# Expert outputs of the small blocks: sums in SBUF by one-hot products in place of scatter-adds to DRAM

## The chip, the core and the metric

The kernel runs on one core of one Trainium2 chip. The metric is the device time of one execution in microseconds (us). Three runs of the kernel before took 1320.86, 1321.10 and 1316.58 us, median 1320.86. One further execution was profiled: its own time was 1310.08 us and the span of its trace, from the first to the last instruction, 1308.3 us. All rows below come from that execution, and times inside the kernel are counted from the start of the span. Engines are called as in the profile: PE (matrix products, with PEld for the loading of their stationary operand), DVE (vector), ACT (scalar), POOL (GpSimd) and SP, which here only issues transfers. PE's granted clock of 1.0 is 2.4 GHz; the other level is half of it, so 0.74 in a window is a mean of the two.

## What is computed

One encoder layer on 512 tokens of width 1024, all in fp32: a layer norm; a mixer (sparse attention and differential attention); a cross attention into 256 memory tokens; and a mixture of experts, with a layer norm after each. The change touches the last part only:

```
scores = sigmoid(x @ router_w);  top_e = top 8 of scores + bias
gates  = scores[top_e] / sum * 2.5
y[t]   = sum over the 8 experts e of t:  gate * ((silu(x Wg[e]) * (x Wu[e])) @ Wd[e])
y[t]  += shared expert of t
out    = layer_norm(ALPHA * x + y)
```

There are 64 routed experts, each with three weights of 1 MiB (gate and up 1024 x 256, down 256 x 1024). All 64 are read in every run, about 201 MB of the 325 MB that the kernel moves.

## The kernel before

The experts are sorted by how many tokens chose them. Rank r gets a fixed room of CAPS[r] rows: 128 to 160 for the first ranks, then 112, 96 and 80, then 64 rows for 19 experts (ranks 38 to 56) and 48 rows for 7 (ranks 57 to 63). Ranks 4 and 5 have room for 160 rows and are two blocks each, one of 128 and one of 32 rows. So there are 66 blocks. They run in the order of rank, except that the two big experts are put in at the places BIG_AT = (30, 50) of the order of experts: the first among the experts of 80 rows, the second among those of 64. Tokens beyond the rooms would go through a loop at the end (`tc.For_i`, line 1590) whose count is read at run time and is zero here.

A block begins with a gather: POOL issues an indirect transfer that fetches the block's rows from DRAM (`gather`, line 1218), two blocks ahead. Transposes on PE turn them (`expert_x`, or `narrow_x` in blocks of up to 64 rows), then come gate and up products, the gate on ACT (line 1299), the product with the gate weight on DVE (hm, line 1304), a transpose of that (`expert_h`), and the down product. Blocks of more than 64 rows ("wide") split weights and rows into a high and a low fp32r part on ACT and DVE and take three products for each (`mm3`, lines 101 to 103). Blocks of at most 64 rows ("narrow", 26 of them) use plain fp32, with gate and up side by side on the two halves of the output partitions (`narrow_mm`, line 1280), and the two halves of the down product likewise (`narrow_out`, line 1291). ACT copies the down product into y (line 1294), and POOL issues an indirect transfer with addition into the DRAM tensor acc, 4 KB a row (`scatter`, line 1332). Rows of the room that hold no token go to spare rows of acc. Each scatter waits until the one before it has landed. acc already holds ALPHA * x plus the shared expert.

Weights are loaded by SP in the order of the blocks (`fetch`, `top_up`), up to LEAD = 9 loads ahead of the one in use. Weights, y, the norm's parameters and most other large tiles share one pool of 20 slots of 8 KB a partition (`slot`); a load can be issued once the slot that it was given has been left by its former tile. Products go to 8 PSUM banks (`bank`).

The order of the work on each engine is the order in which the generators of the code are stepped: `schedule` steps them by the times that they yield. In the last part only `experts` is left, which hands narrow blocks to `narrow_block` (line 1494): six of eight k steps of the products; the transpose of the former block's hm; the last two k steps; the gate; the former block's down product and scatter (`finish`); this block's hm; the transposes of the next block's rows.

After the blocks the overflow loop is passed, the four 128-row tiles of acc are read back (line 1625), normed (lines 1627 to 1641, tiles 1 and 3 with their statistics on ACT) and stored.

Of the kernel before, what the change touches and what calls it, by code (L numbers as in the profile page):

```python
# [10 lines left out]
F32 = mybir.dt.float32  # L11
F32R = mybir.dt.float32r
# [7 lines left out]
P = 128  # L20
# [19 lines left out]
AHEAD, LEAD = 2, 9  # L40
BIG_AT = (30, 50)
GRP = 4
# [16 lines left out]
def encoder_layer(  # L59
# [1222 lines left out]

    def narrow_out(m, ht, wd, n):

        if m % 2 == 0:
            Y["y"] = slot([P, 2, D], name="y")
        y = Y["y"][:, m % 2, :]
        ps = bank()
        for j in range(2):
            for c in range(2):  # L1290
                nc.tensor.matmul(ps[HALF * c:HALF * c + n, :], lhsT=ht[:, j, 0:n], rhs=wd[:, j, c * 512:(c + 1) * 512],
                                 start=j == 0, stop=j == 1)
        for c in range(2):
            nc.scalar.copy(y[0:n, c * 512:(c + 1) * 512], ps[HALF * c:HALF * c + n, :])
        return y

# [97 lines left out]
    metas = [[(r, r, 0) for r in range(a, b)] for a, b in [(0, 2), (2, FIX)]] + metas  # L1394
    NB = len(blocks)
    W, XG, GS = {}, {}, {}

# [83 lines left out]
    def finish(m, ht, n, wd, si):  # L1481
        if narrow(m):
            y = narrow_out(m, ht, wd, n)
        else:
            for c in range(2):
                y = expert_out(m, ht, wd, c, n)
        scatter(y, si, n)

# [5 lines left out]
    def narrow_block(m, X, xt, gs, si):  # L1494
        r, _, n, _ = blocks[m]
        step = 3 * step_of[r]
        ps = bank()
        w = W[r]
        narrow_mm(xt, w, n, ps, range(KH))
        yield 0.45 * KH, 0.0  # L1500
        ht = expert_h(*BEFORE[0][0:2])
        narrow_mm(xt, w, n, ps, range(KH, KD))
        yield 0.9, 0.0
        top_up(step + 2)
        sg = expert_gate(ps, n)
        finish(m - 1, ht, *BEFORE[0][1:])
        yield 1.8, 0.0
        BEFORE[0] = expert_mid(sg, ps[HALF:HALF + n], gs, n), n, w[2], si
        split_part(m + 1, 0)
        if m + 1 < NB:  # L1510
            X[m + 1] = rows_x(m + 1)
        yield 0.8, 0.0
        lists()
        lists()

    def experts():
# [46 lines left out]
        for _ in g_m:  # L1563
            pass
        finish(NB - 1, expert_h(*BEFORE[0][0:2]), *BEFORE[0][1:])

    for u in range(2):
# [22 lines left out]
    with tc.For_i(0, left, 1) as k:  # L1590
# [24 lines left out]
        pu = expert_mm(xt, w3[1])  # L1615
        ht = expert_h(expert_mid(expert_gate(pg), pu, gs))
        for c in range(2):
            y = expert_out(0, ht, w3[2], c)
        scatter(y, si)


    gb = G3[0]
    h3 = [slot([P, 2, D], name="h") for _ in range(2)]
    for t in range(NT):
        nc.sync.dma_start(h3[t // 2][:, t % 2, :], acc[t * P:(t + 1) * P, :])
    st = []
    for t in range(NT):
        h = h3[t // 2][:, t % 2, :]
        if t % 2:
            st.append(act_stats(h))  # L1630
        else:
            mv, rs = row_scale(row_stats(h, 1, row_stats(h, 0)))
            st.append((mv[:, 0:1], rs))
    for t in range(NT):
        h = h3[t // 2][:, t % 2, :]
        mu, rs = st[t]
        hc = [(h[:, cs], gb[:, 0, cs], gb[:, 1, cs]) for cs in (slice(0, 512), slice(512, 1024))]
        for v, g, _ in hc:
            nc.vector.scalar_tensor_tensor(v, v, mu, g, op0=OP.subtract, op1=OP.mult)  # L1639
        for c, (v, _, b) in enumerate(hc):  # L1640
            scale_add(v, v, rs, b, c == 0)
        nc.sync.dma_start(out[0, t * P:(t + 1) * P, :], h)
# [31 lines left out]
```

## Time and profile before

| | |
|---|---|
| median of three runs | 1320.86 us |
| profiled execution, its own time | 1310.08 us |
| its span | 1308.3 us |
| first narrow block's first product | 1011.37 us |
| last output product ends | 1270.15 us |
| first statistics of the last norm | 1289.92 us |
| PE, DVE, ACT, POOL busy | 88%, 57%, 43%, 34% of the span |
| DMA traffic | 324.67 MB, mean 248 GB/s |

The busy shares are means over the whole span. The first 600 us are the attention parts. From about 640 to 1010 us the wide blocks run, from there to 1270 us the narrow ones, and the last 38 us are the scatters that are left, the reading of acc and the norm. In a row of instructions the first number is the start, the second the time from the first start to the last end of the merged instructions, and the bracket tells how long the engine stood idle before and what released it. A merged row is several instructions of one form (x24 is 24). A plain fp32 product appears as two instructions.

### The profile page before, as it was taken

How to read it: one execution, taken by the hardware profiler on the slowest of the kernel's cores; microseconds unless marked ns; L12 is line 12 of the kernel's file. 1: busy time of each engine (PE TensorE's matmuls, PEld its weight loads, DVE VectorE, ACT ScalarE, POOL GpSimd, SP SyncE). 2: the span in 40 equal slices, each digit the busy share in tenths (PEclk: the TensorE clock that was granted, in tenths of full speed). 3: DMA queues.
4: the chain of work that ended last, by engine and by line, in shares of the span. 5: the costliest groups of instructions: out<-in, count | busy, mean ns of one | idle time of the engine just before them, and what ended most of it. 6: DMA issues, size and time to landing. Idle time of an engine off the chain costs nothing. (4 is left out here: it accounts for less than half of the span.)

```text
span 1308.3 us, 20859 instructions
## 1 busy us (share of the span) xinstructions
PE 1155.8 (88%) x7768; PEld 908.2 (69%) x7768; DVE 748.5 (57%) x1617; ACT 562.0 (43%) x1006; POOL 439.5 (34%) x288
## 2 busy tenths in 40 slices
PE   3999999999898899889999999999899988897770
PEld 2887778988898898878778777777667544553330
DVE  7168986566865557787767777666465211311114
ACT  3235456644454453335555556555454211321122
POOL 4333444542236343552212323232213222223213
PEclk9999999998999899999999999999999989998995
DMA  7322234463326256688999999999999999999974
GB/s 225 86 74 65 58 103 114 121 202 116 126 67 210 63 185 208 226 332 329 299 289 331 352 347 362 332 359 359 350 367 338 350 347 387 363 363 353 349 279 141
DMA packets 136807, 324.67 MB, mean 248 GB/s; under 512 B 12001, under 2 KB 94945, under 8 KB 111873
## 3 DMA queue, kind: packets, MB, share of 16 engines
q1 hardware_dynamic: 119984, 275.83, 58.2%
q0 software_dynamic: 13632, 46.80, 14.8%
q8 instruction: 62, 1.02, 0.3%
q10 hardware_dynamic: 3088, 0.69, 0.2%
q14 instruction: 41, 0.33, 0.1%
HBM read 288.10 MB, written 35.19 MB: 247 GB/s over the span
## 5 line engine op out<-in xcount | busy, mean ns | idle before, releaser
L95 POOL TENSOR_TENSOR whl<-wraw,whl 128x1024 fp32r<-128x1024 f32 x81 | 195.9, 2419 | 265.4 <-ACT whl L94 239.4
L1244 DVE TENSOR_TENSOR whl<-wraw,whl 128x1024 fp32r<-128x1024 f32 x152 | 182.9, 1231 | 85.7 <-ACT whl L1243 79.6
L1332 POOL DMA_INDIRECT acc<-y,sidx x66 | 104.8, 1587 | 361.5 <-DMA acc<-y,sidx 161.4
L101 PE MATMUL ps<-whl,xt 128*96 128x256 f32 (+4 forms) x640 | 184.3, 288 | 5.6 <-ACT whl L1243 3.9
L103 PE MATMUL ps<-whl,xt 128*96 128x256 f32 (+4 forms) x640 | 179.8, 281 | 1.9 <-DVE xt L95 1.9
L102 PE MATMUL ps<-whl,xt 128*96 128x256 f32 (+4 forms) x640 | 179.6, 281 | 0.6 <-DVE whl L1244 0.6
L1243 ACT CAST whl<-wraw 128x1024 fp32r<-128x1024 f32 x152 | 152.5, 1053 | 27.9 <-DMA wraw<-in_e_w_gate_dram 20.0
L1327 PE MATMUL ps<-wd,ht 128*96 128x512 f32 (+4 forms) x320 | 147.1, 603 | 4.0 <-DVE ht L1315 3.8
L1280 PE MATMUL ps<-wraw,xn 128*64 128x256 f32 (+1 forms) x832 | 116.8, 404 | 27.0 <-DMA wraw<-in_e_w_up_dram 12.2
L1220 POOL DMA_INDIRECT xg<-rows,gidx x66 | 76.5, 1159 | 160.3 <-PE ps L1252 62.5
L1299 ACT ACTIVATE sg<-ps 64x256 f32<-64x256 f32 (+6 forms) x66 | 25.0, 378 | 239.6 <-PE ps L1280 127.1
L94 ACT CAST whl<-wraw 128x1024 fp32r<-128x1024 f32 x91 | 95.4, 1048 | 57.1 <-PE ps L103 46.5
L101 PEld LDWEIGHTS ps<-whl,xt 128*96 128x96 f32 (+4 forms) x640 | 104.3, 163 | 6.8 <-ACT whl L1243 4.1
L103 PEld LDWEIGHTS ps<-whl,xt 128*96 128x96 f32 (+4 forms) x640 | 104.3, 163 | 2.9 <-DVE xt L95 2.6
L1280 PEld LDWEIGHTS ps<-wraw,xn 128*64 128x64 f32 (+1 forms) x832 | 60.6, 140 | 65.0 <-DMA wraw<-in_e_w_up_dram 15.8
L102 PEld LDWEIGHTS ps<-whl,xt 128*96 128x96 f32 (+4 forms) x640 | 104.5, 163 | 1.1 <-DVE whl L1244 0.7
L1327 PEld LDWEIGHTS ps<-wd,ht 128*96 128x96 f32 (+4 forms) x320 | 49.5, 164 | 72.9 <-issue 66.0
L1315 DVE COPY ht<-ps 128x128 f32<-128x128 f32 (+6 forms) x66 | 21.4, 324 | 96.3 <-PE ps L1313 96.3
L1328 ACT COPY y<-ps 96x512 f32<-96x512 f32 (+4 forms) x80 | 46.3, 582 | 68.8 <-PE ps L1327 67.4
L1304 DVE SCALAR_TENSOR_TENSOR hm<-ps,og,sg 64x256 f32<-64x256 f32 (+4 forms) x54 | 36.8, 681 | 58.0 <-ACT sg L1299 48.8
L101 PE MATMUL ps<-xTh,whl 128*128 128x512 f32 (+1 forms) x168 | 65.6, 390 | 0.0
L103 PE MATMUL ps<-xTh,whl 128*128 128x512 f32 (+1 forms) x168 | 63.8, 380 | 0.0
(421 smaller groups left out, 2756.7 us busy)
## 6 DMA issues: line engine op xcount, KB each, us to landing
wraw<-in_e_w_gate_dram SPq DMA_DIRECT2D x64, 1024.0 KB, 18.8
wraw<-in_e_w_up_dram SPq DMA_DIRECT2D x64, 1024.0 KB, 15.7
wd<-in_e_w_down_dram SPq DMA_DIRECT2D x64, 1024.0 KB, 18.0
wraw<-in_w_in_dram SPq DMA_DIRECT2D x21, 512.0 KB, 3.7
wraw<-in_m_wkv_dram SPq DMA_DIRECT2D x16, 512.0 KB, 4.2
wraw<-in_m_wq_dram SPq DMA_DIRECT2D x16, 512.0 KB, 3.9
wraw<-in_m_wo_dram SPq DMA_DIRECT2D x16, 512.0 KB, 3.9
wraw<-in_w_o_dram SPq DMA_DIRECT2D x12, 512.0 KB, 3.5
```

The costliest lines, as they stand in the source:

```text
L94: nc.scalar.copy(hi, src)
L95: eng.tensor_sub(lo, src, hi.bitcast(F32))
L101: nc.tensor.matmul(ps, lhsT=a, rhs=b, start=start, stop=False)
L102: nc.tensor.matmul(ps, lhsT=a, rhs=bl, start=False, stop=False)
L103: nc.tensor.matmul(ps, lhsT=al, rhs=b, start=False, stop=stop)
L1220: nc.gpsimd.indirect_dma_start(out=xg[0:n, :], out_offset=None, in_=rows, in_offset=bass.IndirectOffsetOnAxis(ap=gi[0:n, :], axis=0))
L1243: nc.scalar.copy(hi[v], w[i][v])
L1244: lo_eng.tensor_sub(lo[v], w[i][v], hi[v].bitcast(F32))
L1280: nc.tensor.matmul(ps[HALF * i:HALF * i + n, 0:256], lhsT=xt[:, k, 0:n], rhs=w[i][:, k, :], start=k == 0, stop=k == KD - 1)
L1327: nc.tensor.matmul(ps[0:n, :], lhsT=ht[:, j, 0:n], rhs=wd[:, j, cs], start=j == 0, stop=j == 1)
L1328: nc.scalar.copy(y[0:n, cs], ps[0:n, :])
L1332: nc.gpsimd.indirect_dma_start(out=acc, out_offset=bass.IndirectOffsetOnAxis(ap=si[0:n, :], axis=0), in_=y[0:n, :], in_offset=None, comput ...
```

## The change

Narrow blocks no longer scatter. Their down products are split into a high and a low fp32r part (yp: the high part by ACT's copies, the low part by DVE), two blocks side by side on the 128 partitions of one tile. From the token numbers of the 128 rows (stf) DVE makes a one-hot matrix, row by token (one_hot_rows: a comparison of 512 columns with the row's number). `add_sums` multiplies its transpose with both parts and adds the result, 128 tokens by 512 columns at a time, to sums in SBUF: eight steps for a pair, each of two products of 512 columns and one DVE addition from PSUM. Steps wait in a list FL, and `flush(2)` takes two of them twice in every narrow block. `flush(16)` takes the rest after the last block.

The sums (ACC, two slots) are read from acc by four transfers on POOL's queue in the third narrow block, after the scatters of the wide blocks. The one-hot tile (ohs, one slot) is made in the second. For this all narrow blocks have to be at the end, so BIG_AT becomes (22, 32): both big experts stand among the wide ones, and an assertion says so. The overflow loop's block adds to the sums in the same way. The last norm reads the sums; the reading back of acc is gone. In `narrow_block` two yields are larger, which moves nothing since no other generator is left then.

```diff
-BIG_AT = (30, 50)
+BIG_AT = (22, 32)
+    def start_sums():
+        OHS[0] = ohs = slot([P, 4, SEQ], F32R, name="ohs")
+        tk = wk([P, SEQ], name="tk")
+        nc.gpsimd.iota(tk, pattern=[[1, SEQ]], base=0, channel_multiplier=0, allow_small_or_imprecise_dtypes=True)
+        nc.vector.tensor_copy(ohs[:, 0, :], tk)
+    def load_sums():
+        for u in range(2):
+            a = slot([P, 2, D], name="sums")
+            for t in range(2):
+                nc.gpsimd.dma_start(a[:, t, :], acc[(2 * u + t) * P:(2 * u + t + 1) * P, :])
+                ACC.append(a[:, t, :])
+    def one_hot_rows(oh, stf):
+        nc.vector.tensor_scalar(oh, OHS[0][:, 0, :].bitcast(F32), stf, None, op0=OP.is_equal)
+    def add_sums(oh, yp):
+        for t in range(NT):
+            for c in range(2):
+                cs = slice(c * 512, (c + 1) * 512)
+                ps = bank()
+                for l in range(2):
+                    nc.tensor.matmul(ps, lhsT=oh[:, t * P:(t + 1) * P], rhs=yp[:, l, cs], start=l == 0, stop=l == 1)
+                nc.vector.tensor_add(ACC[t][:, cs], ACC[t][:, cs], ps)
+                yield
-    def narrow_out(m, ht, wd, n):
-        if m % 2 == 0:
-            Y["y"] = slot([P, 2, D], name="y")
-        y = Y["y"][:, m % 2, :]
+    def narrow_out(m, ht, wd, n, si):
+        i = m - M0
+        p, base = i // 2, HALF * (i % 2)
+        if i % 2 == 0:
+            PAIR[p] = slot([P, 2, D], F32R, name="yp")
+            STF[p] = small.tile([P, 1], F32, name="stf", bufs=3)
+            if min(blocks[m][2], blocks[m + 1][2]) < HALF:
+                nc.vector.memset(STF[p], -1.0)
+        yp, stf = PAIR[p], STF[p]
+        r = slice(base, base + n)
+        if n < HALF:
+            nc.vector.memset(yp[base + 32:base + HALF].bitcast(F32), 0.0)
         ...
+        nc.scalar.copy(stf[r], si[0:n])
         for c in range(2):
-            nc.scalar.copy(y[0:n, c * 512:(c + 1) * 512], ps[HALF * c:HALF * c + n, :])
+            cs, v = slice(c * 512, (c + 1) * 512), ps[HALF * c:HALF * c + n, :]
+            nc.scalar.copy(yp[r, 0, cs], v)
+            nc.vector.tensor_sub(yp[r, 1, cs], v, yp[r, 0, cs].bitcast(F32))
+        if i % 2:
+            oh = OHS[0][:, 1 + p % 3, :]
+            one_hot_rows(oh, STF.pop(p))
+            FL.append(add_sums(oh, PAIR.pop(p)))
     def narrow_block(m, X, xt, gs, si):
+        if m == M0 + 1:
+            start_sums()
+        if m == M0 + 2:
+            load_sums()
         ...
         ht = expert_h(*BEFORE[0][0:2])
+        flush(2)
         narrow_mm(xt, w, n, ps, range(KH, KD))
         ...
         finish(m - 1, ht, *BEFORE[0][1:])
         ...
             X[m + 1] = rows_x(m + 1)
+        flush(2)
         ...
         finish(NB - 1, expert_h(*BEFORE[0][0:2]), *BEFORE[0][1:])
+        flush(16)
-    h3 = [slot([P, 2, D], name="h") for _ in range(2)]
-    for t in range(NT):
-        nc.sync.dma_start(h3[t // 2][:, t % 2, :], acc[t * P:(t + 1) * P, :])
     ...
-        h = h3[t // 2][:, t % 2, :]
+        h = ACC[t]
```

M0 is the number of the first narrow block.

## Rows read from the trace of the kernel before

**Rows 1.** The page, busy tenths in 40 slices of 32.7 us

```profile
PE   3999999999898899889999999999899988897770
...
DMA  7322234463326256688999999999999999999974
```

**Rows 2.** Windows: PE, PEld, DVE, ACT, POOL busy; clock, DMA share, GB/s

```profile
800.00:820.00 20.00, 19.96 (x146) 15.95 (x145) 15.26 (x29) 12.07 (x18) 6.90 (x4) 1.00 1.03 347
...
1200.00:1220.00 20.00, 15.22 (x86) 7.32 (x88) 1.58 (x4) 1.07 (x3) 4.67 (x4) 0.74 1.02 339
```

**Rows 3.** PE's waits from 700 to 1000 us: us, times, longest

```profile
PE ps L1313 <- DVE sidx L1185: 4.7, 1, 4.7
```

**Rows 4.** PE's waits from 1000 to 1270 us

```profile
PE ps L1280 <- DMA wraw<-in_e_w_up_dram: 12.2, 7, 3.2
```

**Rows 5.** Waits of the load queue from 640 to 1270 us

```profile
SPq L1226 <- DMA acc<-y,sidx: 199.7, 16, 16.2
```

**Rows 6.** The DMA queues from 1000 to 1260 us; last column: us to landing

```profile
DMA packets 15178, 94.13 MB, mean 362 GB/s; under 512 B 2053, under 2 KB 2053, under 8 KB 5349
...
q1 hardware_dynamic: 11039, 80.37, 80.4%
q0 software_dynamic: 4120, 13.50, 21.6%
...
xg<-rows,gidx POOLq DMA_INDIRECT x26, 8.7
```

**Rows 7.** The timeline of all engines from 1225 to 1310 us

```profile
1259.78 0.63 PE L1280 MATMUL ps<-wraw,xn 128*48 128x256 f32 x2 [0.20 <-ACT xn L1273]
...
1267.34 1.35 POOL L1332 DMA_INDIRECT acc<-y,sidx  x1 [4.62 <-ACT sg L1299]
...
1268.23 1.92 PE L1291 MATMUL ps<-wd,ht 128*48 128x512 f32 x8 [0.35 <-DVE ht L1315]
...
1281.80 1.35 POOL L1332 DMA_INDIRECT acc<-y,sidx  x1 [3.41 <-DMA acc<-y,sidx]
...
1289.92 1.28 DVE L171 BATCH_NORM_STATS2 st<-h 128x6 f32<-128x512 f32 x2 [21.74 <-DMA h<-acc]
```

**Rows 8.** The timeline of PE from 1008 to 1060 us

```profile
1011.37 2.81 PE L1280 MATMUL ps<-wraw,xn 128*64 128x256 f32 x24
...
1037.68 2.81 PE L1280 MATMUL ps<-wraw,xn 128*64 128x256 f32 x24 [1.02 <-ACT xn L1273]
...
1044.39 2.81 PE L1280 MATMUL ps<-wraw,xn 128*64 128x256 f32 x24 [0.26 <-ACT xn L1273]
...
1051.86 2.81 PE L1280 MATMUL ps<-wraw,xn 128*64 128x256 f32 x24 [1.03 <-ACT xn L1273]
```

**Rows 9.** Window of one scatter alone, columns as in rows 2

```profile
1272.20:1277.00 4.80, 0.00 (x0) 0.00 (x0) 0.00 (x0) 0.00 (x0) 1.35 (x1) 0.80 0.30 43
```

**Rows 10.** The timeline of PE from 100 us, twelve products in a row

```profile
100.11 0.40 PE L101 MATMUL ps<-xTh,whl 128*128 128x512 f32 x1
...
102.64 0.39 PE L103 MATMUL ps<-xTh,whl 128*128 128x512 f32 x1
```

**Rows 11.** PE's timeline in the wide stage, transposes of x

```profile
917.89 1.04 PE L1252 MATMUL ps<-ident,xg 128*128 128x128 f32 x8
...
939.14 0.72 PE L1252 MATMUL ps<-ident,xg 80*128 80x80 f32 x8
```

**Rows 12.** DVE's instructions by line and form: busy us, mean ns, idle

```profile
L1304 DVE SCALAR_TENSOR_TENSOR hm<-ps,og,sg 64x256 f32<-64x256 f32 x19 | 12.8, 672 | 24.7 <-ACT sg L1299 24.6
...
L95 DVE TENSOR_TENSOR x<-ps,x 128x512 fp32r<-128x512 f32 x16 | 10.4, 677 | 0.0
...
L1271 DVE COPY xn<-ps 128x256 f32<-128x256 f32 x19 | 8.1, 424 | 47.9 <-PE ps L1268 47.9
...
L1190 DVE TENSOR_TENSOR oh<-slot_id,rt 128x512 fp32r<-128x512 f32 x6 | 3.9, 678 | 0.0
...
L166 DVE MEMSET kz<- 64x1024 f32 x2 | 1.8, 912 | 0.4 <-issue 0.4
```

More of the change, by code (lines that the diff above doesn't have):

```diff
@@ L1281, in narrow_mm @@
                                  start=k == 0, stop=k == KD - 1)
-    def narrow_out(m, ht, wd, n):
-        if m % 2 == 0:
-            Y["y"] = slot([P, 2, D], name="y")
-        y = Y["y"][:, m % 2, :]
+    ACC, PAIR, STF, OHS, FL = [], {}, {}, {}, []
+    def start_sums():
[32 more added lines that the diff above has]
+            nc.vector.memset(yp[base + 32:base + HALF].bitcast(F32), 0.0)
         ps = bank()
@@ L1292, in narrow_out, with flush @@
                                  start=j == 0, stop=j == 1)
+        nc.scalar.copy(stf[r], si[0:n])
         for c in range(2):
-            nc.scalar.copy(y[0:n, c * 512:(c + 1) * 512], ps[HALF * c:HALF * c + n, :])
-        return y
+            cs, v = slice(c * 512, (c + 1) * 512), ps[HALF * c:HALF * c + n, :]
[5 more added lines that the diff above has]
+            FL.append(add_sums(oh, PAIR.pop(p)))
+    def flush(n):
+        while n and FL:
+            if next(FL[0], 0) == 0:
+                FL.pop(0)
+            else:
+                n -= 1
     def expert_gate(pg, n=P):
@@ L1395, in encoder_layer @@
     NB = len(blocks)
+    M0 = min(m for m in range(NB) if blocks[m][2] <= HALF and not blocks[m][1])
+    assert all(blocks[m][2] <= HALF and not blocks[m][1] for m in range(M0, NB)) and (NB - M0) % 2 == 0
     W, XG, GS = {}, {}, {}
@@ L1482, in finish @@
         if narrow(m):
-            y = narrow_out(m, ht, wd, n)
+            narrow_out(m, ht, wd, n, si)
         else:
@@ L1486, in finish @@
                 y = expert_out(m, ht, wd, c, n)
-        scatter(y, si, n)
+            scatter(y, si, n)
     def rows_x(m):
@@ L1501, in narrow_block @@
         ht = expert_h(*BEFORE[0][0:2])
+        flush(2)
         narrow_mm(xt, w, n, ps, range(KH, KD))
-        yield 0.9, 0.0
+        yield 1.8, 0.0
         top_up(step + 2)
@@ L1511, in narrow_block @@
             X[m + 1] = rows_x(m + 1)
-        yield 0.8, 0.0
+        flush(2)
+        yield 1.6, 0.0
         lists()
@@ L1616, in encoder_layer @@
         ht = expert_h(expert_mid(expert_gate(pg), pu, gs))
-        for c in range(2):
-            y = expert_out(0, ht, w3[2], c)
-        scatter(y, si)
+        stf = small.tile([P, 1], F32, name="stf", bufs=3)
+        nc.vector.tensor_copy(stf, si)
+        oh = OHS[0][:, 1, :]
+        one_hot_rows(oh, stf)
+        yp = slot([P, 2, D], F32R, name="yp")
+        for c in range(2):
+            cs = slice(c * 512, (c + 1) * 512)
+            ps = bank()
+            for j in range(2):
+                nc.tensor.matmul(ps, lhsT=ht[:, j, :], rhs=w3[2][:, j, cs], start=j == 0, stop=j == 1)
+            split(yp[:, 0, cs], yp[:, 1, cs], ps)
+        for _ in add_sums(oh, yp):
+            pass
     gb = G3[0]
-    h3 = [slot([P, 2, D], name="h") for _ in range(2)]
-    for t in range(NT):
-        nc.sync.dma_start(h3[t // 2][:, t % 2, :], acc[t * P:(t + 1) * P, :])
     st = []
     for t in range(NT):
-        h = h3[t // 2][:, t % 2, :]
+        h = ACC[t]
         if t % 2:
@@ L1634, in encoder_layer @@
     for t in range(NT):
-        h = h3[t // 2][:, t % 2, :]
+        h = ACC[t]
         mu, rs = st[t]
```

## The prediction

> **What bounds the kernel now.** I read the page's forty slices first, then the windows, the DMA queues by stretch, the waits of PE and of the load queue, and last the timelines of both ends of the narrow stage (the 26 experts of at most 64 rows). In the slices the DMA line stands at 9 from slice 20 (about 620 us) to slice 38 (1240 us), while PE falls to 8 and 7 toward the end [rows 1]. The windows say the same by numbers: at 800 us PE and DMA are both full (19.96 of 20 us, share 1.03); at 1200 us PE has 15.22 us and a granted clock of 0.74, with the DMA share unchanged at 1.02 [rows 2]. In the wide stage PE sets the pace: over 300 us the longest of its waits there, 4.7 us, is for a DVE list and none is for a transfer [rows 3]. In the narrow stage PE does wait for weights (12.2 us for the up weights alone, the rest appearing as slow clock and small gaps) [rows 4], so loads set the pace there. They are not slowed by their own bytes only: the queue that issues them stood 199.7 us in all waiting for a scatter-add to land, because the next slot still held a y [rows 5]; and indirect transfers took 21.6% of the engines' time for 13.50 of 94.13 MB [rows 6]. After the last narrow product (1268.23 us plus 1.92) four scatters follow one another, 1267.34 to 1281.80, each behind the landing of the one before; the layer norm's first statistics start at 1289.92, 19.8 us after PE ended, and the norm with its stores takes the 18.4 us that are left of the span [rows 7].
>
> So the narrow stage runs from 1011.37 [rows 8] to 1270.15 us: 258.8 us for 26 narrow blocks and the second big expert (128 + 32 rows), which stands among them.
>
> **What the change does to the loads.** Removed: 19 x 64 + 7 x 48 = 1552 scattered rows. Plain loads move 80.37 MB in 80.4% of 260 us, 384 GB/s. At that rate the gathered half of the 13.50 MB costs 17.6 of the 56.2 us of the indirect queue; 38.6 us are left for 1648 scattered rows, 23.4 ns each [rows 6]. An undisturbed 48-row scatter gives 0.30 x 4.8 us = 1.44 us, 30 ns a row [rows 9], so 23.4 is not too high. 1552 rows then free 36 us of the engines. Added: four plain loads of the sums, 2.1 MB, 5.5 us at 384 GB/s. Net: 31 us less DMA work in the narrow stage. Lower bound: if only bytes count, 6.36 - 2.10 MB at the 362 GB/s of the stretch [rows 6], 12 us.
>
> The Trainium skill ("DMA: Bandwidth & Descriptors", Specifications) puts the HBM share of one core at about 358 GB/s. The stretch's 362 GB/s sits at that figure; by it, the removal would be worth its bytes only, the 12 us, loads rather than PE would end the stage, and the sum would be 12 - 2 + 9.5, 1301 us. That speaks against the larger gain, and no row of before shows plain loads alone in this stage.
>
> **What it does to PE.** Where loads were ahead, narrow blocks follow one another 6.71 and 7.47 us apart, with a wait for ACT's xn of 0.26 and 1.03 us in them: 6.45 us of products [rows 8]. Added are 16 fp32r products of 512 columns per pair, eight per block. In the input projection the same form starts every 0.230 us (100.11 to 102.64, eleven steps) [rows 10]: 1.84 us. Half of them stand right after the transposes of x, in the gap that waited for xn, so of that wait I keep 0.2. A block: 6.45 + 1.84 + 0.2 = 8.5 us, with 8.3 and 9.3 (the full gap kept) as ends.
>
> BIG_AT takes the big expert out of the narrow stage and puts it among the wide ones. There its two blocks cost what the first big expert's do, 917.89 to 939.14, 21.25 us of PE [rows 11]; the narrow blocks start that much later, at 1032.6. Its loads (3.1 MB, 160 rows each way) come to about 13.6 us by the prices above, so the loads gain some 7 us of lead there, not a loss. Below-nothing bound: if the wide stage had slack, up to 8 us cheaper. Moving the first big one eight places changes no sum.
>
> End of the stage: before, from the last block's first product to the end of the last output product, 1259.78 to 1270.15, are 10.4 us [rows 7]; with one flush of four products 11.3. 1032.6 + 25 x 8.5 + 11.3 = 1256.4, against 1270.15: 13.7 us earlier. The loads alone would allow 12 to 31 us, so PE and the loads end together; the smaller decides.
>
> **DVE and ACT.** A block gets four PSUM adds and two splits (a 128x512 subtract from PSUM is 677 ns; for the 64-row form I take the same), half a one-hot (678 ns at the tensor-tensor form; I take 0.5 us, from 0.3 to 0.7), beside hm 672 and xn 424 ns [rows 12]: 4 x 0.68 + 2 x 0.68 + 0.25 + 0.67 + 0.42 and 0.3 for ht = 5.7 us of 8.5. PE and DVE run beside each other, so I cost this at nothing; without that cover it is the slow rival below. The memset of the seven 48-row halves (0.912 us for 64x1024, so some 1.8 for their 2048 columns [rows 12]) lies under the output products. ACT loses nothing but a small copy of the indices; its two output copies stay.
>
> **The added wait.** The sums load behind the last wide scatter on POOL's queue; gathers stand behind them. A gather lands in 8.7 us here [rows 6]. The loads are issued two blocks (17 us) after that scatter's block began and the first add comes about 7 us later, so DVE may stand some microseconds at its first add, with hm and xn behind it and PE behind those: 0 to 9 us, once. I take 2 us, since the load lead covers the rest. Three slots are held to the end (two of sums, one of one-hots). I count 12 weights, up to 3 pairs, these 3 and the norm's parameters: 19 of 20, so loads are not starved but wait for PE instead of for scatters.
>
> **The tail.** Before: 19.8 us. After: the two copies and splits 2.0, one-hot 0.5, then the adds still open. Each block flushes four of a pair's eight steps, so two of the last but one pair and eight of the last remain: 10 x 0.68 = 6.8 us on DVE, PE beside it. To this 2 us for stepping over the empty overflow loop, which earlier lay under the scatters (0.7 to 5). Together 11.3: 8.5 earlier (5 to 10). The norm then finds all rows at once rather than as transfers land; I take 1 us of its 18.4 (0 to 2).
>
> **Sum.** 13.7 - 2 + 8.5 + 1 = 21 us. The profiled execution took 1310.08 us (span 1308.3 and 1.8 around it), so it would take 1289. The median shown, 1320.86, lies 10.8 above that execution; I move it by the same 21: 1300 us.
>
> **Rivals.**
> 1. Only the tail is won: loads are held by their bytes, or the first adds stall, and the stage ends where it ended: 1321 - 9.5 = 1311.5. For it: the flat 362 GB/s. Against: 199.7 us of load issues behind scatters, and 23.4 ns a row.
> 2. More is won: PE's gap is filled wholly (8.3 us a block, 5 us), no stall (2), an overflow step of 0.7 (1.3), lead kept, wide stage some 2 cheaper: 1290. For it: 31 us of freed engine time.
> 3. Slower: DVE in its fixed order becomes part of PE's chain. If hm or xn of a block stand behind two adds that wait for products which PE has behind them, each block costs 2 x 0.68 = 1.36 us more, 9.9 us; 25 x 1.36 = 34 us, 1334. It decides from 21 / 25 = 0.84 us a block. For it: DVE's queue is in order and eight banks serve about nine uses a block. Against: only 5.7 of 8.5 us are busy, and by the order of the code xn is ready before the second half of the products needs it.
> 4. Loads starve for slots: the same place, the count of 19 exceeded; a block at its 8.2 us of weights plus a late issue of 2 us costs 10.2 us, 25 x 1.7 = 42 us more than forecast, 1342. Against: nothing long-lived beyond the count.
>
> **Chances.** Forecast 0.50 (its own range 1294 to 1307), rival 1 0.20, rival 2 0.17, rivals 3 and 4 0.13 together. 0.5% is 6.6 us, about what a measurement here can tell from no change. Rival 1 lies near that line, so half of it goes to no change, and 0.03 of the slow ones: faster 0.77, same 0.13, slower 0.10. The range 1285 to 1319 leaves out most of rivals 3 and 4 and the ends of the others.
>
> **What would show it.** Narrow blocks 8.3 to 8.8 us apart with PE near full and granted clock 1.0; indirect traffic of a stretch there halved; load issues no longer waiting for scatters; the norm's first statistics 10 to 12 us after the last output product. Blocks 9.4 us or more apart, with PE waiting for xn, hm or a bank, or first statistics over 19 us after the last output product, would make the prediction wrong.

## The result, and the profile after

The changed kernel is slower: 1354.83 us (median of four runs, 1351.25 to 1360.13) against 1319.61 for the kernel before beside it, a ratio of 1.0272 (95% interval 1.0240 to 1.0304). The profiled execution took 1351.25 us, its span is 1349.4. The profiled execution of before was 9.5 us under its own median, so the spans differ by 41.1 us where the medians differ by 35.2; below, spans are compared with spans. One of the four runs of one experiment (1359.77 us; fixed slots, loads 7 ahead, no fill) took over 1.5% longer than the fastest of its kernel and is left out of that kernel's median and ratio.

Two stretches of the page of after first, the busy tenths that answer to [rows 1].

```profile
PE   3999999999897999889999999799999899889781
...
PEclk9999999999899999999999999799999899999896
DMA  6322234464235257779899999999999999998601
```

PE now stands at 8 and 9 almost to the end, where it had fallen to 7, and the DMA line falls before PE does. The windows, with the columns of [rows 2], give the numbers.

```profile
800.00:820.00 20.00, 19.96 (x144) 16.04 (x143) 14.10 (x28) 12.00 (x18) 6.78 (x4) 1.00 1.03 342
860.00:880.00 20.00, 10.39 (x45) 5.33 (x44) 8.68 (x15) 8.74 (x15) 2.73 (x3) 0.66 1.03 358
1160.00:1180.00 20.00, 18.21 (x116) 9.55 (x114) 11.32 (x24) 3.73 (x10) 1.79 (x2) 1.00 0.94 333
1200.00:1220.00 20.00, 18.21 (x116) 9.75 (x116) 11.51 (x24) 4.10 (x10) 1.76 (x2) 1.00 0.91 334
```

At 1200 us PE has 18.21 of 20 us at full clock where it had 15.22 at a clock of 0.74, and the DMA share is 0.91 where it was 1.02: loads no longer set the pace there; PE does, with what it waits for. What PE waits for from 1040 to 1310 us (us, times, longest) has changed altogether; the 12.2 us for weights of [rows 4] are gone.

```profile
PE ps L1310 <- ACT yp L1335: 14.7, 8, 4.0
PE ps L1310 <- DVE yp L1336: 9.4, 12, 3.5
```

L1310 is the one-hot product, L1335 and L1336 make the high and low part that it reads. The load queue (from 1000 us on) now waits for products, and for scatters only 11.7 us:

```profile
SPq L1226 <- PE ps L1280: 108.4, 20, 14.5
...
SPq L1226 <- PE ps L1310: 42.9, 9, 5.3
```

This must not be set against the 199.7 us of [rows 5]. Those are counted from 640 us on, and 167.5 of them lie before 1000 us, behind the scatters of the wide blocks, which stay. From 1000 to 1270 us the load queue of the kernel before stood this long for scatters:

```profile
SPq L1226 <- DMA acc<-y,sidx: 32.1, 3, 13.4
SPq L1235 <- DMA acc<-y,sidx: 19.6, 2, 16.1
```

So the transfers were relieved, though of less than [rows 5] seemed to say, and the time went to PE's side. The starts of the transposes of x show how: the narrow blocks follow one another 6.8, 6.8, 17.3, 8.6, 10.9, 8.6, 10.8, 8.7, 12.8, 8.6 and then 11.8 and 8.6 in turn, with 15.3 and 15.9 for the long ones of the last pairs. Every second block takes 8.6 us, as forecast (8.5); the other one does not. One of each, on PE:

```profile
1199.88 0.71 PE L1268 MATMUL ps<-ident,xg 64*128 64x64 f32 x8
...
1200.52 1.21 PE L1310 MATMUL ps<-yp,ohs 128*128 128x512 f32 x4
...
1201.66 2.81 PE L1280 MATMUL ps<-wraw,xn 128*64 128x256 f32 x24
...
1208.53 0.71 PE L1268 MATMUL ps<-ident,xg 64*128 64x64 f32 x8
...
1210.58 0.49 PE L1310 MATMUL ps<-yp,ohs 128*128 128x512 f32 x1 [1.34 <-ACT yp L1335]
1211.41 1.11 PE L1310 MATMUL ps<-yp,ohs 128*128 128x512 f32 x2 [0.34 <-DVE yp L1336]
1212.45 1.51 PE L1280 MATMUL ps<-wraw,xn 128*64 128x256 f32 x10
1213.89 0.49 PE L1310 MATMUL ps<-yp,ohs 128*128 128x512 f32 x1
...
1220.31 0.71 PE L1268 MATMUL ps<-ident,xg 64*128 64x64 f32 x8
```

In the first block four products of an older pair stand in 1.14 us behind the transposes. In the second the four products belong to a pair whose output products have only just ended, and PE reaches them before the parts exist. The fourth even stands behind ten gate and up instructions (five products). ACT's timeline shows that the parts come late for a second reason (the first line is the output product of the even block):

```profile
1198.06 1.89 PE L1330 MATMUL ps<-wd,ht 128*64 128x512 f32 x8
...
1209.08 0.37 ACT L1273 COPY xn<-ps 128x256 f32<-128x256 f32 x1 [0.59 <-PE ps L1268]
1209.35 2.62 ACT L1335 CAST yp<-ps 64x512 fp32r<-64x512 f32 x4
```

Four casts stand in one row: the two of the even block, whose output product ended at 1199.95 us, are made only together with those of the odd block.

The tail answers to [rows 7]: the last output product ends at 1312.15 + 1.92 = 1314.07, and DVE's first statistics start at 1324.51.

```profile
1312.15 1.92 PE L1330 MATMUL ps<-wd,ht 128*48 128x512 f32 x8 [1.42 <-DVE ht L1368]
...
1316.23 4.09 PE L1310 MATMUL ps<-yp,ohs 128*128 128x512 f32 x15 [0.80 <-DVE yp L1336]
...
1324.51 0.69 DVE L171 BATCH_NORM_STATS2 st<-sums 128x6 f32<-128x512 f32 x1 [1.84 <-issue]
```

These are 10.4 us instead of 19.8. But from there to the end of the span it is 24.9 us instead of 18.4.

### The profile page after: what moved, and what is told of

Same layout as the page of the kernel before. It is cut to its first block, busy times and chain, and to the rows that moved or that the text cites. A ratio compares the mean times of both kernels' runs of the same rounds, so it can differ in the third digit from the quotient of the medians.

```text
span 1349.4 us, 21384 instructions
## 1 busy us (share of the span) xinstructions
PE 1215.1 (90%) x7976; PEld 943.0 (70%) x7976; DVE 868.9 (64%) x1798; ACT 567.0 (42%) x1032; POOL 408.0 (30%) x267
## 3 DMA queue, kind: packets, MB, share of 16 engines
q0 software_dynamic: 12240, 42.54, 12.4%
## 5 line engine op out<-in xcount | busy, mean ns | idle before, releaser
L1220 POOL DMA_INDIRECT xg<-rows,gidx x66 | 80.3, 1216 | 328.4 <-PE ps L1268 201.6
L1243 ACT CAST whl<-wraw 128x1024 fp32r<-128x1024 f32 x152 | 152.2, 1054 | 11.7 <-DMA acc<-y,sidx 10.4
L1385 POOL DMA_INDIRECT acc<-y,sidx x40 | 66.8, 1670 | 200.2 <-DMA acc<-y,sidx 62.4
L1310 PE MATMUL ps<-yp,ohs 128*128 128x512 f32 x208 | 73.4, 450 | 26.5 <-ACT yp L1335 14.7
L1311 DVE TENSOR_TENSOR sums<-sums,ps 128x512 f32<-128x512 f32 x104 | 67.9, 684 | 34.3 <-PE ps L1310 27.9
L1280 PEld LDWEIGHTS ps<-wraw,xn 128*64 128x64 f32 (+1 forms) x832 | 57.5, 137 | 46.5 <-issue 22.0
L1310 PEld LDWEIGHTS ps<-yp,ohs 128*128 128x128 f32 x208 | 37.0, 192 | 50.7 <-ACT yp L1335 21.9
L101 PE MATMUL ps<-xTh,whl 128*128 128x512 f32 (+1 forms) x168 | 65.5, 390 | 0.0
```

The costliest lines, as they stand in the source:

```text
L101: nc.tensor.matmul(ps, lhsT=a, rhs=b, start=start, stop=False)
L1220: nc.gpsimd.indirect_dma_start(out=xg[0:n, :], out_offset=None, in_=rows, in_offset=bass.IndirectOffsetOnAxis(ap=gi[0:n, :], axis=0))
L1243: nc.scalar.copy(hi[v], w[i][v])
L1280: nc.tensor.matmul(ps[HALF * i:HALF * i + n, 0:256], lhsT=xt[:, k, 0:n], rhs=w[i][:, k, :], start=k == 0, stop=k == KD - 1)
L1310: nc.tensor.matmul(ps, lhsT=oh[:, t * P:(t + 1) * P], rhs=yp[:, l, cs], start=l == 0, stop=l == 1)
L1311: nc.vector.tensor_add(ACC[t][:, cs], ACC[t][:, cs], ps)
```

## The experiments

All ratios are to the kernel before, run on the same chip beside them (medians 1318.7 to 1319.3 us). "Pair" means two narrow blocks whose outputs share one yp.

### First set: the parts of the change

**Later addition.** Theory A: the fresh pair's products are reached too early. A finished pair is put on the list of open steps one block later.

```diff
-            FL.append(add_sums(oh, PAIR.pop(p)))
+            NEW.append(add_sums(oh, PAIR.pop(p)))
     def narrow_block(m, X, xt, gs, si):
+        FL.extend(NEW)
+        NEW.clear()
```

> The changed kernel, with one edit: a finished pair enters the list of steps one block later, so no product is asked for in the block that makes its operand; twelve steps instead of ten are left for the end. Theory A (the time goes to flushes of a pair whose split has only just begun, PE waiting in order): the narrow blocks come 8.6 us apart throughout instead of 8.6 and 10.8 to 15.9 in turn; 25 intervals lose 35 to 40 us, the first add's stall shrinks, the tail gains 1.4 us: 1312 to 1322. Rival B (loads are the next bound at about 9.3 us a block, as the share of 0.93 at 10.2 us suggests): 1328 to 1338. Rival C (the products and adds cost that much wherever they stand): 1350 to 1358.

Measured: 1361.89 us, ratio 1.0331 (1.0304 to 1.0359), above all three ranges. Theory A, alone, falls. The intervals of the first pairs did come down (8.0 to 9.9 us), but later the long ones were 13 to 18 us, and PE waited for ACT's casts as before:

```profile
PE ps L1310 <- ACT yp L1335: 16.2, 7, 4.4
PE ps L1310 <- DVE yp L1336: 4.7, 7, 0.8
```

**The big experts moved, nothing else**, in the kernel before.

```diff
-BIG_AT = (30, 50)
+BIG_AT = (22, 32)
```

> The kernel before, with BIG_AT = (22, 32) alone. Theory A with the working of the prediction: the wide stage gets 21 us longer and the narrow one, paced by loads, 14 us shorter: 1322 to 1330. Rival D (the move itself is what costs, as the first narrow product came 28 us later in the changed kernel): 1340 to 1350.

Measured: 1328.76 us, ratio 1.0099 (1.0062 to 1.0136). The move by itself costs about 10 us. The first narrow product starts at 1040.0 us, 28.6 later than at [rows 8]; the forecast was 21.25. The time is in theory A's range: the narrow stage (1040.0 to 1283.45) is 15.4 us shorter, about the 14 expected. It cannot give back more: PE waits 25.5 us for the gate weights alone.

**No narrow scatters** in the kernel before (the outputs of the narrow blocks are left out of the sums).

```diff
-        scatter(y, si, n)
+        if not narrow(m):
+            scatter(y, si, n)
```

> The kernel before without the scatters of the 26 narrow blocks (their outputs are left out of the sums). It prices what the change could win at most from transfers. With 23 ns a scattered row as in the prediction: 36 us of load time and about 10 us of the tail, 1275 to 1285. If only bytes count: 17 us and the tail, 1290 to 1297.

Measured: 1286.51 us, ratio 0.9750 (0.9713 to 0.9787), between the two ranges. The relief that the change is after exists, and is about 32 us, tail included.

**No products and additions** in the kernel after (splits, one-hots and the loading of the sums stay; the outputs of the narrow blocks are left out).

```diff
     def flush(n):
-        while n and FL:
...
+        FL.clear()
```

> The changed kernel with all splits, one-hots and loads of sums, but the one-hot products and their adds left out (the narrow outputs do not reach the sums). Theory A: without products nothing waits for a fresh split, PE needs about 7 us a block and loads set the pace at 9 or so: 1295 to 1308. Rival E (the splits on ACT and DVE with their fills are the delay, products or not): above 1330.

Measured: 1325.79 us, ratio 1.0036 (0.9998 to 1.0075), between the two ranges. So 29 us come with the products and additions. Without them the kernel is still 7 us above before, though 32 us of relief are in it: if these effects add, which was not tried, 10 of the 39 are the big experts' places, and 29 go with what is left in, splits, fills, one-hots and the loading of the sums. By the waits it is work on DVE: PE stands 24.8 us for ht and 14.1 for hm.

### Second set: slots

Theory F: the 20 slots are all in use (12 weights, 2 of sums, 1 of one-hots, up to 3 yp, and the two tables rt and rv that the overflow loop still needs), so a new yp gets its place late and the even block's casts are put off. In three kernels that is undone or eased.

**Three slots for yp taken once**, and used in turn.

```diff
+        YPS.extend(slot([P, 2, D], F32R, name="yps") for _ in range(3))
...
-            PAIR[p] = slot([P, 2, D], F32R, name="yp")
+            PAIR[p] = YPS[p % 3]
```

> The kernel after with one edit: yp is no longer taken anew from the pool of 20 slots for every pair; three slots are taken once, beside ohs, and the pairs take them in turn. In the order of ACT's instructions as it is built, the even block's two casts then stand after its own output product and no longer behind the rows of the block after next together with the odd block's (in the kernel after four casts stand in one row from the fourth pair on). Theory F (a new yp gets its slot late, so that four casts and four subtractions stand in one row and PE's next products wait for them): the long intervals between blocks fall from 11.7 us to 8.6 us, about 3.2 us in each of some 11 pairs and 5 us more in the last two, and the time is 1310 to 1325 (ratio to before 0.995 to 1.005). Rival G (loads: the 20 slots are still full, the wait only moves to the loads): PE waits for wraw instead, and the time is 1340 to 1355. Rival H (the work of DVE and ACT itself): the long intervals stay at 11 us or spread over both blocks, 1345 to 1360.

Measured: 1356.67 us, ratio 1.0267 (1.0224 to 1.0310), in rival H's range. Theory F, alone, falls too. The casts are in their places and PE's wait for them is gone, but in the middle of the stage the long interval only went from 11.8 to 10.9 us, and toward the end the short one rose from 8.6 to 9.4: the narrow stage (1050.14 to 1324.59) takes 274.5 us, as in the kernel after. Now PE waits for the subtraction of the fresh pair, as its timeline shows:

```profile
1199.26 1.11 PE L1311 MATMUL ps<-yps,ohs 128*128 128x512 f32 x2 [0.70 <-DVE yps L1337]
...
1200.31 1.51 PE L1280 MATMUL ps<-wraw,xn 128*64 128x256 f32 x10
...
1201.75 0.50 PE L1311 MATMUL ps<-yps,ohs 128*128 128x512 f32 x1
```

**Loads 6 ahead instead of 9** in the narrow stage, yp from the pool.

```diff
-        while fetched[0] < min(max(used + LEAD, ahead), 3 * NEXP):
+        while fetched[0] < min(max(used + (6 if LATE[0] else LEAD), ahead if not LATE[0] else 0), 3 * NEXP):
...
+        LATE[0] = 1
```

> The kernel after with one edit: once the narrow blocks have begun, weights are requested 6 loads ahead of the one in use and not 9, so that three of the 20 slots are free for yp; yp is taken from the pool as before. In the order as it is built the casts of the first six pairs stand after their own products, and from the seventh pair on four stand in one row, as in the kernel after. Theory F: only the first six pairs gain their 3.2 us each, 1330 to 1342. Rival G (loads come too late): less lead makes it worse or leaves it, 1352 to 1365, with PE waiting for wraw. Rival H: no change, 1350 to 1358.

Measured: 1367.65 us, ratio 1.0377 (1.0348 to 1.0406), worse, and above all three ranges. Rival G's sign was right but not its reason: PE waits for no weights in this stage, and again 16.8 us for ACT's casts: from the fifth pair on, and not only from the seventh, the casts of the even block come together with those of the odd one. In the first four pairs, whose casts are in their places, the long intervals are 10.8 to 10.9 us, so those gained 1 us against the 11.8 of the kernel after and not 3.2. And since three loads fewer did not bring the later casts to their places, it is not shown that the number of slots alone makes yp late.

**Fixed slots, loads 7 ahead, no fill.** A third edit: the idle rows of yp in pairs with a 48-row block are not filled since they hold older finite values and their one-hot columns are zero.

```diff
-        if n < HALF:
-            nc.vector.memset(yp[base + 32:base + HALF].bitcast(F32), 0.0)
```

> As the run with three fixed slots for yp, and two edits more: weights are requested 7 loads ahead once the narrow blocks have begun (so that slots are left), and the fill of the idle rows of yp in the pairs with a 48-row block is gone, since these rows hold older finite products and their one-hot columns are zero. Theory F: against the run with fixed slots alone about 0 to -8 us (four fills of 1.76 us in the last pairs, some of them in DVE's way): 1305 to 1322. Rival H (DVE's own work): -8 to -14 against the run with fixed slots alone, from the last three pairs only. Rival G: worse than with fixed slots alone by 5 us or more, from waits for wraw.

Measured: 1341.44 us, ratio 1.0177 (1.0141 to 1.0212), 15.2 less than with fixed slots alone, more than theory F's 8 and rival H's 14. What the lead and the fill each gave is not told apart by this run.

**The same with the later addition.**

> As the run before it in this list, and a finished pair is added one block later (it goes to the list of pending steps at the start of the next block and not at once), so that the first pair's addition has its sums in time. Theory F: the first addition's wait of 5.9 us (an interval of 17.3 us instead of 8.6) goes; with the casts in order the later pairs have their parts ready, so no interval is above 9.5 us: 1296 to 1314. Rival (what the late list did alone, +7 us, was its own doing): no better than the run without it, 1305 to 1325.

Measured: 1333.53 us, ratio 1.0126 (1.0091 to 1.0162). The two edits that had each done nothing alone are worth 21 us together with the lead and the fill, 8 of them against the run before this one. But the expected 1296 to 1314 was missed: from the ninth interval on all of them, of both kinds, were 9.4 to 10.3 us, with PE in another order. One block on PE's timeline:

```profile
1189.06 0.70 PE L1268 MATMUL ps<-ident,xg 64*128 64x64 f32 x8
1189.70 1.20 PE L1311 MATMUL ps<-yps,ohs 128*128 128x512 f32 x4
1190.83 0.65 PE L1280 MATMUL ps<-wraw,xn 128*64 128x256 f32 x2
1191.40 0.33 PE L1365 MATMUL ps<-ident,hm 64*128 64x64 f32 x2
1191.66 1.20 PE L1311 MATMUL ps<-yps,ohs 128*128 128x512 f32 x4
1193.31 1.50 PE L1329 MATMUL ps<-wd,ht 128*64 128x512 f32 x5 [0.45 <-DVE ht L1367]
```

As written, 24 gate and up instructions stand between the two groups of one-hot products, and cover the making of hm and ht. Here one product (two instructions) does. The program that lays out the instructions had put the rest behind, presumably since it reckoned with late up weights; no run shows its reason. In the instruction orders (T transposes of x, P one-hot products, M gate and up products, H transposes of hm, D output products):

```
as written                        T8 P4 M12 H2 P4 M4 D4
built, fixed slots + late addition T8 P4 M1 H2 P4 D3 M15 D1
```

### Third set: all three, and one left out at a time

**All three edits**: fixed slots (two suffice now), later addition, and PE's order tied down. Loads are 9 ahead, the fill is left out.

```diff
-        narrow_mm(xt, w, n, ps, range(KH))
+        last = narrow_mm(xt, w, n, ps, range(KH))
         yield 0.45 * KH, 0.0
-        ht = expert_h(*BEFORE[0][0:2])
-        flush(2)
+        with tc.issue_after(last.ins):
+            ht = expert_h(*BEFORE[0][0:2])
+            flush(2)
```

The same is done for `finish` behind the last two k steps.

> The three edits together: yp in fixed slots (two suffice, taken once), a finished pair is added one block later, and PE's order is tied down: the transposes of hm and the products of the sums stand behind the first six k steps of a block, the output products behind the last two, as the code is written (in the run with fixed slots and late addition the built order is: four products, one k step of gate, hm, four products, three of four output products, and only then the other 15 gate and up products, since the builder reckons with late loads). Loads are 9 ahead as in the kernel after. Theory (two waits and an order, each of which alone holds the odd blocks at 10 to 11 us): all intervals between blocks 8.6 us, as the even blocks show in the kernel after, 1.1 us less than the 9.85 us of the run with fixed slots and late addition, so 25 to 28 us off that run's 1333.5: 1303 to 1310. Rival (the loads now limit): a block reads 3.15 MB of weights and up to 0.26 MB of rows, at 375 to 383 GB/s 8.9 to 9.1 us, PE waits for wraw, 1312 to 1322. Rival (the wide stage's stall is longer with slots taken): first narrow product at 1050 and not 1043, and the time 7 us above either.

Measured: 1312.47 us, ratio 0.9956 (0.9925 to 0.9988): 42 us less than the kernel after, and 0.4% below the kernel before, with an interval that just leaves out no change. The time lies just above the theory's range and at the lower end of the first rival's. The intervals are 6.8 to 8.0 us for the first three, then 8.6 (one of 10.2) up to 1153 us and 8.6 to 9.2 (one of 10.0) after it. The two stretches in windows:

```profile
1100.00:1160.00 60.00, 60.00 (x404) 34.14 (x402) 40.16 (x83) 14.21 (x35) 6.29 (x7) 1.00 1.02 368
1160.00:1240.00 80.00, 79.17 (x514) 46.45 (x511) 48.54 (x96) 17.22 (x40) 7.94 (x9) 1.00 1.02 378
```

PE and the DMA engines are both full. In the second stretch the rival has its share: a block's 3.15 MB of weights and 0.26 MB of rows at 378 GB/s are 9.0 us, there the load queue waits for hardly anything but earlier loads, and the 24 gate and up instructions at 1172 and 1181 us take 3.15 and 3.26 us, where those at 1111 us took 2.81.

**Without the later addition** (three fixed slots, order tied down, no fill).

```diff
-            NEW.append(add_sums(oh, PAIR.pop(p)))
+            FL.append(add_sums(oh, PAIR.pop(p)))
```

> The same without the later addition (a finished pair's first four products stand in the block in which its last part is made), three fixed slots, PE's order tied down. If the fresh pair is a wait of its own: intervals 8.6 and 10.8 in turn, narrow stage 2.2 us times 13 = 28 us longer than with the later addition, 1335 to 1350. If the order on PE was the whole trouble: no difference between the two, both at 1303 to 1315.

Measured: 1348.64 us, ratio 1.0230 (1.0196 to 1.0264); intervals 8.6 and 10.8 to 12.4 in turn, and PE's waits are for the fresh pair's low part:

```profile
PE ps L1312 <- DVE yps L1336: 14.6, 17, 4.8
```

**Without the fixed slots** (later addition, order tied down, filled).

```diff
-            PAIR[p] = YPS[p % 2]
+            PAIR[p] = slot([P, 2, D], F32R, name="yp")
```

> Two of the three edits: a finished pair is added one block later, and PE's order is tied down; yp is taken from the pool of 20 slots for every pair, as in the kernel after, and its idle rows are filled. In the order as built the casts of a pair's four parts stand in one row from the fourth pair on. Theory (all three are needed): the long intervals stay, 13 to 15 us in the later pairs as in the run with the later addition alone, 1350 to 1365. Rival (slots don't matter once PE's order is right): 1310 to 1320.

Measured: 1361.32 us, ratio 1.0296 (1.0233 to 1.0360); later long intervals of 13 to 18 us, 16.4 us of waiting for ACT's casts.

**With the fill** (all three edits).

```diff
+        if n < HALF:
+            nc.vector.memset(yp[base + 32:base + HALF].bitcast(F32), 0.0)
```

> All three edits, with the fill of the idle rows of yp kept (two fills in each pair's life where a block has 48 rows, 1.76 us of DVE each). Theory (DVE has room: 11 to 14 of 20 us busy in these stretches): within 3 us of the version without the fill, 1310 to 1316. Rival (DVE's own work costs in the 48-row pairs, where intervals of 13.9 to 14.2 us were seen with the fill and fixed slots): 8 to 14 us more, 1320 to 1327.

Measured: 1318.40 us, ratio 0.9991 (0.9955 to 1.0028). The fill costs about 5 us, between the two expectations; the long intervals of the last pairs are 10.5 us with it.

**Big experts at places 30 and 36** (all three edits, no fill).

```diff
-BIG_AT = (22, 32)
+BIG_AT = (30, 36)
```

> The first of this list with the two big experts at places 30 and 36 of the order and not at 22 and 32 (both still among the wide ones). Theory (the 10 us that moving the big experts cost by itself come from the place: the first big expert's split waits at 860 to 875 us for a slot that an output held until its scatter landed, behind scatters of 96 rows): the stall of 7 to 11 us is gone or smaller, since the scatters at place 30 have 80 rows: 6 to 10 us faster than the first of this list. Rival (any place among the wide ones costs this, since two big blocks near the end leave their scatters in the way of the loading of the sums): within 3 us, or slower.

Measured: 1310.36 us, ratio 0.9921 (0.9896 to 0.9945). That is 2 us from the version at (22, 32): the rival held, and this is the fastest version that computes the whole layer, by less than can be told apart. The first narrow product starts at 1046.1 us, against 1044.3, and PE's longest wait in the wide stage is 13.6 us, against 9.1: the stall is not gone.

**No overflow loop** (all three edits, no fill).

```diff
-    with tc.For_i(0, left, 1) as k:
...
```

> The version with all three edits (1312.5 us), and the overflow loop after the blocks left out (its count is read at run time and is zero here; so a part of the computation that no token needs in this run is left out). In every version without narrow scatters the span ends 25.9 to 26.4 us after the first statistics of the last norm, and the last 6 us of it hold no instruction's work: SP waits for PE's sequencer at the kernel's last line; in the kernel before it is 18.4 us. Theory (what ends last is a fixed length of PE's own way from the loop that all engines pass together to the end of the program, about 26 us, which in the kernel before lay beside the scatters and the reading of acc): without the loop the statistics start as soon as the first sums are final and the end follows the last store as before, 6 us from the end and 1 to 3 us from the start: 1302 to 1307. Rival (the 6 us belong to the end of the program as such, to semaphores or stores that are late): 1310 to 1313.

Measured: 1312.91 us, ratio 0.9938 (0.9907 to 0.9969). The time is the one with the loop, and my theory of the tail falls. In the profiled executions the norm's last vector instruction ends 2.3 us earlier and the span 2.4, but 24.9 us still lie between the first statistics and the end, as with the loop (24.5 to 25.0 us in all traces without narrow scatters, and not the 25.9 to 26.4 of my expectation). In the waits of the load queue the same one stands as in the versions with the loop. The profile puts it down to PE's sequencer; the part on the tail below shows that it is another:

```profile
SPq L1700 <- PEq L1700: 6.6, 2, 6.1
```

## Why the prediction was wrong

The forecast put the span at 1308.3 - 21 = 1287.3 us; it came out at 1349.4, 62.1 more. By its own steps:

| step | forecast | measured | more |
|---|---|---|---|
| first narrow product | 1032.6 | 1039.60 | 7.0 |
| the first addition's stall | 2 | 17.3 - 10.9 = 6.4 | 4.4 |
| the other narrow blocks, to the end of the last output product | 223.8 | 274.5 - 6.4 = 268.1 | 44.3 |
| from there to the first statistics | 11.3 | 10.4 | -0.9 |
| norm and end | 17.4 | 24.9 | 7.5 |

The sum is 62.3. The stall is taken against 10.9 us since the block that it falls in is one of the long ones.

**The step that failed most** is the block of 8.5 us with DVE and ACT "at nothing", together with the sentence that half of the one-hot products stand "in the gap that waited for xn". The 8.5 itself was right: it is the 8.6 of every second block, and of nearly all blocks up to 1153 us with the three edits. What was not looked at is which pair's products stand in that gap. In every second block it is the pair just finished, and between its output product and its first one-hot product lie a cast, a subtraction, another cast and another subtraction, none of them covered. A busy sum of 5.7 of 8.5 us says nothing about such a chain. Rival 3 was the right kind (DVE in its order inside PE's chain, 1334 us), but it named hm and xn and not the parts of yp.

**The count of slots** was the second. "19 of 20" left out rt and rv, which live to the overflow loop: with them there are 21 tiles for 20 slots. Rival 4 expected that loads would starve; they did not (PE waits for no weights after 1040 us). It was yp that came late, so the casts of two blocks stood in a row; with yp in fixed slots they did not. That the count is what made it late is argued from the code.

These two held the long interval each by itself. Removing either one alone left 1356.67 or 1361.89 us, and only when both were gone did the long intervals go. (With fixed slots but no later addition, other edits brought the time to 1341.44 and 1348.64 us, but the run of 1348.64 us still has long intervals of 10.8 us and more.) That is also why the first two theories fell when tested alone. The third, the order on PE, appeared only when the first two were gone: 1333.53 without it against 1312.47 with it, a difference that also holds the lead (7 and 9) and the count of yp's slots (3 and 2). With all three in place, leaving out the later addition costs 36 us (with three slots in the place of two) and taking yp from the pool (with the fill, so compared with 1318.40) 43. The narrow stage of the version with all three takes 1274.23 - 1044.33 = 229.9 us, for a forecast of 225.8 with the stall.

**The first addition** was bounded at 0 to 9 us and I took 2, on the ground that the load lead covers the rest. It took 6.4, inside the bounds: the lead is in weights, and what stood still was DVE.

```profile
1068.58 0.69 DVE L1311 TENSOR_TENSOR sums<-sums,ps 128x512 f32<-128x512 f32 x1 [5.90 <-DMA sums<-acc]
```

**The big expert** cost 28.2 us and not 21.25. Most of the rest is a longer stall at the first big expert, where a split's slot still held an output whose scatter had not landed: ACT stood, DVE's half of the split behind it, and hm on DVE and PE behind that (ACT's and PE's waits from 840 to 890 us):

```profile
ACT whl L1243 <- DMA acc<-y,sidx: 10.4, 1, 10.4
```

```profile
PE ps L1366 <- DVE sidx L1185: 9.6, 1, 9.6
```

The granted clock in 860 to 880 us is 0.66 (a mean of both levels) beside it. The kernel before has the same stall at its first big expert: PE's 4.7 us of [rows 3] ended at 949.8 us, behind a wait of ACT of 5.4 us for a scatter. The prediction read that row as a wait for a list, and "none is for a transfer", so it priced the move without it. The one other pair of places that was tried did not bring the time back.

**The relief of the loads** was there, but less than the 31 us forecast. Without narrow scatters the kernel before takes 32 us less; its narrow stage (1015.79 to 1255.31) is 19.3 us shorter, between the bounds of 12 and 31, and the stretch from the last output product to the end 9.0. The waits that were counted for it, the 199.7 us of [rows 5], belonged to the wide stage for the most part. The Trainium skill ("DMA: Bandwidth & Descriptors", Specifications) gives one core about 358 GB/s of HBM, half of what two cores share; here one core runs, and the figure is not the ceiling of this stage, since the version with three edits moves 378 GB/s over 80 us (the windows above).

**The tail's** 10.4 us to the first statistics came as forecast (11.3). The end did not: 24.9 us for a forecast of 17.4. What stands last is POOL's drain at the kernel's last line. The rows of that line give the shortest, median and longest duration in ns, and the first and last start; first before, then after:

```profile
L1669 POOLq DRAIN  x3: 46/104/4055, 1301.3 to 1308.0; - x3
```

```profile
L1738 POOLq DRAIN  x3: 46/104/11132, 1337.5 to 1349.2; - x3
L1738 SPq DRAIN  x3: 7/7/13, 1342.4 to 1348.9; - x3
L1738 PEldq DRAIN  x2: 8/8/8, 1323.7 to 1348.9; - x2
```

The long drain starts first. Before, it ends at 1305.3 us, and the last store lands after it. In the kernel after it ends at 1348.6, 0.8 us before the end of the span. The load queue, at its own drain from 1342.4 us on, then waits 6.3 us, to 0.2 us behind the end of POOL's. The profile names PE's sequencer for this wait, but that had come to the last line at 1323.7. The drain takes 11.13 to 11.15 us in all fourteen traces whose narrow blocks don't scatter, the one without the overflow loop among them, and 4.06 and 4.09 us in the two whose narrow blocks do. Why it is longer there no run shows.

What stays open besides is the part of the fill and of the lead in the run of 1341.44 us, and why the wide stage with two big experts stalls at both pairs of places.

## What to carry to other kernels

Work that is handed to an engine "in its gaps" has to be followed back to what makes its operands: where the gap stands right behind the producer, the engine waits in order, whatever the busy shares say. When two waits end at the same place, undoing either one shows nothing, so an experiment that undoes one and measures no change does not clear it; undo both, then put back one at a time. And where tiles come from a pool, look at the order of instructions as built: here taking yp from the pool put four casts in a row that the code has apart. It is worth counting every tile that lives to the end, those of a loop that is never entered too, though no run here shows what the count alone does.

## What the runs showed of the hardware

- Four one-hot products of 512 columns, with the 128 columns of their stationary operand loaded anew for each, take 1.12 to 1.14 us before the next products. The first takes 0.34 us; the others start 0.23 to 0.24 us apart, as the row of the input projection gave (0.230 [rows 10]). Eight in a block are some 0.4 us more than the 1.84 forecast; the 8.6 us held because no wait for xn was left.
- From 1160 to 1240 us of the version with three edits the core moves 378 GB/s at a DMA share of 1.02, with gathers of 64 and 48 rows among the loads; in the kernel before, with scatters among them too, it was 361 GB/s over 1060 to 1240 us at the same share.
- POOL's drain at the end of the program takes 11.13 to 11.15 us in the traces without narrow scatters and 4.06 and 4.09 us in those with them. In the former the span ends 0.8 us behind it, 24.5 to 25.0 us after the norm's first statistics.
